# Eight more turns of the expert-weight ring, in tiles of G already multiplied

## The chip, the core and the metric

The kernel runs on one core of a Trainium2 chip. The metric is the device time of one execution in microseconds, as the median of several runs; lower is better. Before the change it is 1753.32 us (three runs, 1751.4 to 1754.4). The profile is of one further execution.

## The reference, cut to what matters

One layer of a hybrid encoder is computed for 384 tokens: 128 of eight short sequences and 256 of a prompt. The front of the layer (modulation, projections, RWKV-7 mixing, sparse attention, output projection) takes no part in the change. The layer ends in PEER, a mixture of 16,384 tiny experts with eight heads of sixteen picks each. For every token `n` with normed input `h` of 1024 numbers:

```python
act = gelu(einsum('nhkd,nd->nhk', peer_u[e], h))        # e: 8 x 16 picked experts of a token
out = einsum('nhk,nhkd->nd', g * act, peer_v[e])        # g: softmax of the picks' scores
x = x + g2 * out
```

## The kernel before

Tokens are handled in two ways. The 128 tokens of the short sequences (block 0) go the *sparse* way: for each of a token's 128 picks GpSimd gathers a row of `puv` (the expert's `u` and `v`, 2048 numbers a token, 1 MB for all 128 tokens) into one of three buffers of `raw` (`ring`, L1468). VectorE multiplies the `u` half by `h` and sums (L1593, called the product below), ScalarE turns the sum into a weighted activation (L1594, L1595), and VectorE adds that multiple of the `v` half to `acc` (L1599, the accumulation). One product and one accumulation are a pair; there are 128.

The 256 tokens of the prompt (blocks 1 and 2) go the *dense* way: all experts are computed, 128 tiles of 128 experts. `dense_u` (L1484) loads a tile of `puT`, 512 KB, multiplies it with the tokens on TensorE into the PSUM bank `fx` and puts the gelu into `G[:, j]` for the first 76 tiles, or into `gA` or `gO` for the later 52. A stage in between (`weights`, L1403) multiplies the tiles of G by the routing weights, and writes the weights of the later tiles to DRAM. In the last stage `dense_v` (L1507) loads a tile of `pv`, 512 KB, and multiplies it by the tile of G (or by `gA`, or by `gB` read back from DRAM, after GpSimd has multiplied it by the weights `Ws`), adding up in the four PSUM banks `bx`, `cp`, `dx`, `dx` over all 128 tiles. 36 of the 128 tiles (*whole*) are multiplied as they are, 8 passes each; 92 (*split*) are first cut into a high and a low half for three products of reduced precision: ScalarE makes `wh` and `Gh` (L231), VectorE `wl` and `Gl` (L235), and TensorE runs 12 matmuls. The last 20 tiles are all split. Buffers: four of `wh`, three of `wl`, three of `Gh` and `Gl`.

`expert` (L1473) takes the buffer for a tile of `puT` or `pv` from the ring `w`, four buffers of 128 x 1024, and issues the load on SP's DMA queue. The same queue carries the reads of `Ws` (L1556) and `gB` (L1515) and the writes of `y` (L1571), in order. The last stage is the loop at L1734 over the tiles in a fixed order `order`, which mixes later tiles in among the first 76. In each turn it draws about 0.62 gathers (`pull(SR[2])`), computes ahead the `dense_u` of later tiles (21 are left for this stage), and calls `dense_v`. A gather also waits for the matmuls of the tile five turns back (`self.pace`, L1735). At turn 122 it writes down the residual of block 0, which reads `acc`: two products on VectorE (L1569) and two additions on GpSimd (L1570). The two last tiles are multiplied bank by bank in `finish_v`, and blocks 1 and 2 follow with products and additions on VectorE. The buffers for these residuals are taken from the ring `raw` too, so they come free as the last gathers are used up and the output of block 0 is written.

What order the instructions have on each engine is not set by this code alone: the program is built with `schedule_with_timeline_sim=True`, that is, a scheduler lays the instructions of all engines along a simulated timeline, subject to their dependencies and buffers, and writes each engine's list in that order. At run time every engine takes its list strictly in order, waiting on semaphores.

Of the kernel before, what the change touches and what calls it, by code (L numbers as in the profile page):

```python
# [2 lines left out]

# [178 lines left out]
S0, PH = 30, 4  # L183
OFF = [j for j in range(NW, 128) if (j - NW + 1) * NB // (128 - NW) > (j - NW) * NB // (128 - NW)]
AHEAD = sorted(OFF + [j for j in range(NW, 128) if j not in OFF][:NA - 1])
LAST, EARLY = 126, 108
WB, EB = (4, 4, 3), 3
UENG, VENG, GENG, VN = 'v', 'v', 'g', 3
SENG = 'gv'
# [7 lines left out]
class K:  # L197
    def __init__(self, ctx, tc, I, O):
        self.ctx, self.tc, self.nc, self.I, self.O = ctx, tc, tc.nc, I, O
        self.uid = 0  # L200
        self.const = self.open(ctx, "const")
        self.stream = self.open(ctx, "stream")
        self.dram = self.open(ctx, "dram", space=bass.MemoryType.DRAM)
        self.nlo = 0
        self.lo_pattern = "v"

    def open(self, ctx, name, **kw):
# [1264 lines left out]

    def expert(self, src):  # L1473

        w = self.t([128, 1024], tag="w", bufs=WB[0], pool=self.stream)
        self.nc.sync.dma_start(w, src)
        return w

# [124 lines left out]
    def run(self):  # L1603
# [79 lines left out]
        def pull(rate):  # L1683
            sn[0] += rate
            while sn[0] >= 1:
                sn[0] -= 1
                next(sparse, None)
# [46 lines left out]
        for n, j in enumerate(order):  # L1734
            self.pace = self.vdone[n - 5] if n > 4 else None  # L1735
            pull(SR[2])
            while todo and sum(u not in OFF for u in gs) < NA - 1:
                u = todo.pop(0)
                gs[u] = self.dense_u(u)
            last.append(self.dense_v(j, gs.pop(j) if j >= NW else self.G[:, j], out, n))  # L1740
            if n == 122:
                for _ in sparse:
                    pass
                (a, b), (y, _) = self.ring(), self.ring()
                self.residual(0, [self.acc[:, c * 512:c * 512 + 512] for c in range(2)], self.gate2(0, a), self.x1_rows(0, b), y)
                (a, b), (c, y1), (y2, _) = (self.ring() for _ in range(3))
                g, x1, y = self.gate2(1, a), [self.x1_rows(1, b), self.x1_rows(2, c)], (y1, y2)
# [28 lines left out]
```

## Time and profile before

| | |
|---|---|
| median of three runs | 1753.32 us (1751.4 to 1754.4) |
| the profiled execution | 1746.57 us |
| its span, first to last instruction | 1744.3 us |
| granted TensorE clock, mean over the span | 0.983 |
| TensorE busy (PE) | 1672.7 us, 96% |
| VectorE busy (DVE) | 1352.8 us, 78% |
| ScalarE busy (ACT) | 747.1 us, 43% |
| GpSimd busy (POOL) | 557.4 us, 32% |
| moved by DMA | 437.22 MB, mean 251 GB/s |

In the rows of the profile PE is TensorE's matmul, PEld its load of weights (which overlaps PE), SPq the DMA queue of SP. `out<-in` names the written and the read tiles. A row of waits reads "engine, what waited <- what it waited for: us in total, times, the longest". In a row of the timeline stand the start and the length in us, the engine, the line and the operation, and in brackets how long the engine was idle before it and what ended that. The chain of waits lists pieces by start and length; a piece "DMA raw" runs from a gather's issue to the instruction that needed it. A DMA share of 1.00 means that all 16 DMA engines of the core were busy.

### The profile page before, as it was taken

Reading aid. Unit: us, or ns where it says so; the run is one execution under the profiler, and the core shown is the slowest. Engines: PE = TensorE matmul, PEld = TensorE weight load, DVE = VectorE, ACT = ScalarE, POOL = GpSimd, SP = SyncE. Lnnn points to the kernel's source line nnn. Section 1 sums busy time; section 2 is a strip of 40 time slices with the busy share of each in tenths; the row PEclk is TensorE's granted clock in tenths of the full one; section 3 lists DMA queues with packets and bytes.
Section 4 is the critical chain, followed back from the end, with each engine's and each line's share of the span. In section 5 each row is a group of like instructions: output and inputs, shape, how many; then the busy total and the mean of one; then the engine's idle time right before and its main releaser. Section 6 shows DMA issues by size and latency. Waiting matters only on the chain.

```text
span 1744.3 us, 33104 instructions
## 1 busy us (share of the span) xinstructions
PE 1672.7 (96%) x12376; PEld 1410.9 (81%) x12376; DVE 1352.8 (78%) x2905; ACT 747.1 (43%) x1666; POOL 557.4 (32%) x621
## 2 busy tenths in 40 slices
PE   6999999999999989999999989999999999999998
PEld 4998788878878877999887889999976667767766
DVE  4548788878858865566999998899958777878787
ACT  4443343334343333444323254577853343343344
POOL 2434243343323220035033223342243224333242
PEclk8999899999999999999999999999999999999999
DMA  8543653455365365755498989996579999999995
GB/s 301 165 139 100 196 176 89 146 171 162 104 204 158 96 207 191 257 184 198 126 360 315 370 318 373 387 340 240 176 259 388 346 346 382 382 359 377 349 377 213
DMA packets 173048, 437.22 MB, mean 251 GB/s; under 512 B 46036, under 2 KB 86612, under 8 KB 156504
## 3 DMA queue, kind: packets, MB, share of 16 engines
q1 hardware_dynamic: 154456, 300.89, 50.9%
q0 software_dynamic: 18432, 134.23, 19.9%
q8 instruction: 97, 1.59, 0.4%
q14 instruction: 63, 0.52, 0.1%
HBM read 403.75 MB, written 31.30 MB: 249 GB/s over the span
## 4 chain that ended last, share of the span: by engine, by line
PE 66%; DVE 15%; DMA 9%; issue 4%; ACT 3%; POOL 2%; SPq 0%; DVEq 0%; POOLq 0%; ACTq 0%
PE mm L227 25%; PE fx L227 14%; PE dx L227 11%; PE cp L227 7%; PE bx L227 7%; DMA raw<-in_puv,pe 3%; DVE raw L1593 2%; DVE acc L1599 2%; DVE wl L235 2%; DMA w<-in_pv 2%; DMA w<-in_w_ada 1%; ACT wh L231 1%; DVE psi L1323 1%; DVE ps L1324 1%; DMA w<-in_puT 1%
## 5 line engine op out<-in xcount | busy, mean ns | idle before, releaser
L235 DVE TENSOR_TENSOR wl<-w,wh 128x1024 fp32r<-128x1024 f32 (+1 forms) x274 | 345.7, 1271 | 107.1 <-ACT wh L231 68.0
L231 ACT ACTIVATE wh<-w 128x1024 fp32r<-128x1024 f32 (+1 forms) x282 | 294.9, 1052 | 152.3 <-PE mm L227 71.0
L1586 POOL DMA_INDIRECT raw<-in_puv,pe x128 | 175.2, 1369 | 434.8 <-PE dx L227 159.4
L227 PE MATMUL fx<-h2h,wl 128*128 128x256 f32 x688 | 195.2, 284 | 4.3 <-DVE wl L235 4.3
L227 PE MATMUL fx<-h2h,wh 128*128 128x256 f32 x688 | 196.8, 286 | 1.3 <-ACT wh L231 1.1
L227 PE MATMUL fx<-h2l,wh 128*128 128x256 f32 x688 | 193.1, 281 | 0.0
L1599 DVE SCALAR_TENSOR_TENSOR acc<-raw,dots,acc 128x1024 f32<-128x1024 f32 x127 | 166.6, 1311 | 15.9 <-ACT dots L1595 15.6
L1593 DVE SCALAR_TENSOR_TENSOR raw<-raw,sh 128x1024 f32<-128x1024 f32 x128 | 159.3, 1245 | 18.5 <-DMA raw<-in_puv,pe 14.9
L227 PEld LDWEIGHTS fx<-h2h,wl 128*128 128x128 f32 x688 | 129.9, 189 | 7.3 <-DVE wl L235 6.5
L227 PEld LDWEIGHTS fx<-h2h,wh 128*128 128x128 f32 x688 | 129.8, 189 | 5.0 <-ACT wh L231 2.7
L227 PEld LDWEIGHTS fx<-h2l,wh 128*128 128x128 f32 x688 | 129.9, 189 | 2.0 <-issue 1.5
L227 PE MATMUL mm<-LTh,wh 128*128 128x384 f32 (+2 forms) x352 | 123.7, 352 | 1.6 <-ACT wh L231 1.1
L227 PE MATMUL mm<-LTl,wh 128*128 128x384 f32 (+2 forms) x352 | 122.1, 347 | 1.1 <-POOL LTl L488 1.1
L227 PE MATMUL mm<-LTh,wl 128*128 128x384 f32 (+2 forms) x352 | 122.6, 348 | 0.0
L1594 ACT ACTIVATE dots<-dots 128x1 f32<-128x1 f32 x128 | 25.7, 200 | 189.9 <-DVE raw L1593 189.5
L227 PE MATMUL mm<-h2f,w 128*128 128x256 f32 x464 | 105.4, 381 | 0.0
L227 PE MATMUL mm<-wh,LTh 128*128 128x256 f32 x336 | 99.0, 295 | 1.6 <-ACT qx L891 1.6
L227 PE MATMUL mm<-wl,LTh 128*128 128x256 f32 x336 | 99.9, 297 | 0.0
L227 PE MATMUL mm<-wh,LTl 128*128 128x256 f32 x336 | 98.8, 294 | 0.0
L227 PEld LDWEIGHTS mm<-h2f,w 128*128 128x128 f32 x464 | 87.5, 190 | 12.4
L227 PE MATMUL fx<-h2f,w 128*128 128x256 f32 x336 | 78.0, 385 | 0.0
L227 PEld LDWEIGHTS mm<-LTh,wh 128*128 128x128 f32 (+2 forms) x352 | 66.4, 189 | 7.1 <-issue 2.0
(584 smaller groups left out, 4271.6 us busy)
## 6 DMA issues: line engine op xcount, KB each, us to landing
w<-in_puT SPq DMA_DIRECT2D x128, 512.0 KB
w<-in_pv SPq DMA_DIRECT2D x128, 512.0 KB
w<-in_w_in SPq DMA_DIRECT2D x70, 512.0 KB
w<-in_w_ada SPq DMA_DIRECT2D x48, 512.0 KB
cKT<-in_cKT SPq DMA_DIRECT2D x32, 256.0 KB
cV<-in_cV SPq DMA_DIRECT2D x32, 256.0 KB
w<-in_w_pq SPq DMA_DIRECT2D x16, 512.0 KB
d<-wst SPq DMA_DIRECT2D x8, 832.0 KB
```

Source lines behind the costliest of these rows:

```text
L227: return self.nc.tensor.matmul(out, l, r, start=start, stop=stop, skip_group_check=True, **kw)
L231: self.nc.scalar.activation(hi, src, AF.Copy)
L235: (self.nc.vector if eng == "v" else self.nc.gpsimd).tensor_tensor(lo, src, hi, op=OP.subtract)
L1323: nc.vector.max_index(si[:, half, h, 0:8], sv[:, half, h, 0:8], s[:, c])
L1324: nc.vector.match_replace(out=s2, in_to_replace=sv[:, half, h, 0:8], in_values=s[:, c], imm_value=MARK)
L1586: d = nc.gpsimd.indirect_dma_start(out=bass.AP(tensor=u.tensor, offset=u.offset, ap=[u.ap[0], [1, 2048]]), out_offset=None, in_=self.I["puv"],
L1593: nc.vector.scalar_tensor_tensor(u, u, 1.0, h2, op0=OP.mult, op1=OP.mult, accum_out=dot)
L1594: nc.scalar.activation(dot, dot, AF.Gelu_apprx_tanh)
L1599: nc.vector.scalar_tensor_tensor(acc, v, dot, acc, op0=OP.mult, op1=OP.add)
```

## The change

The ring gets further members. `slots` is a queue that holds None four times, for the four buffers of `w`. `expert` takes its first entry and puts it back at the end; None means a buffer of `w` as before, a number s the four tiles `G[:, 4s:4s+4]`, which together have a buffer's 128 x 1024 numbers. In the last stage, after the tiles up to j = 31 have been passed to `dense_v`, each full four of them adds its number to the queue, so that it grows from four to twelve entries. The queue is walked while the program is built.

```diff
--- before.py
+++ after.py
@@ -1,5 +1,6 @@
 
 import math
+from collections import deque
 from contextlib import ExitStack, nullcontext
 
 import numpy as np
@@ -183,7 +184,7 @@
 S0, PH = 30, 4
 OFF = [j for j in range(NW, 128) if (j - NW + 1) * NB // (128 - NW) > (j - NW) * NB // (128 - NW)]
 AHEAD = sorted(OFF + [j for j in range(NW, 128) if j not in OFF][:NA - 1])
-LAST, EARLY = 126, 108
+LAST, EARLY, SLOTS = 126, 108, 8
 WB, EB = (4, 4, 3), 3
 UENG, VENG, GENG, VN = 'v', 'v', 'g', 3
 SENG = 'gv'
@@ -202,6 +203,7 @@
         self.stream = self.open(ctx, "stream")
         self.dram = self.open(ctx, "dram", space=bass.MemoryType.DRAM)
         self.nlo = 0
+        self.slots = deque([None] * WB[0])
         self.lo_pattern = "v"
 
     def open(self, ctx, name, **kw):
@@ -1472,7 +1474,12 @@
 
     def expert(self, src):
 
-        w = self.t([128, 1024], tag="w", bufs=WB[0], pool=self.stream)
+        s = self.slots.popleft()
+        self.slots.append(s)
+        if s is None:
+            w = self.t([128, 1024], tag="w", bufs=WB[0], pool=self.stream)
+        else:
+            w = self.G[:, 4 * s:4 * s + 4].rearrange("p a b -> p (a b)")
         self.nc.sync.dma_start(w, src)
         return w
 
@@ -1738,6 +1745,8 @@
                 u = todo.pop(0)
                 gs[u] = self.dense_u(u)
             last.append(self.dense_v(j, gs.pop(j) if j >= NW else self.G[:, j], out, n))
+            if j < 4 * SLOTS and j % 4 == 3:
+                self.slots.append(j // 4)
             if n == 122:
                 for _ in sparse:
                     pass
```

The lines of the changed kernel stand 7 lower in this stage (L1593 is L1600 there, L1599 is L1606, L235 is L237, L1476 is L1483).

The scheduler writes another order for all engines from the first load into G on. On SP's DMA queue, early in the last stage, before the change (`w` is the ring, `Ws` and `gB` are read back from DRAM):

```order
L1476 DMA w_2983_15611<-in_pv 128x1024
L1476 DMA w_2990_15641<-in_puT 128x1024
L1476 DMA w_2995_15674<-in_pv 128x1024
L1556 DMA Ws_3128_16275<-d2173_11077 128x8x128
L1476 DMA w_3000_15696<-in_pv 128x1024
L1476 DMA w_3005_15714<-in_pv 128x1024
L1476 DMA w_3012_15743<-in_pv 128x1024
L1476 DMA w_3017_15765<-in_pv 128x1024
L1476 DMA w_3020_15779<-in_puT 128x1024
L1476 DMA w_3025_15812<-in_pv 128x1024
```

The same part after the change:

```order
L1483 DMA G_2172_11076<-in_pv 128x1024
L1563 DMA Ws_3113_16260<-d2173_11077 128x8x128
L1483 DMA w_3008_15739<-in_pv 128x1024
L1483 DMA w_3013_15761<-in_pv 128x1024
L1483 DMA w_3016_15775<-in_puT 128x1024
L1483 DMA G_2172_11076<-in_pv 128x1024 x3
L1483 DMA w_3027_15836<-in_pv 128x1024
L1522 DMA gB_3056_15975<-d2174_11078 128x256
L1483 DMA w_3039_15894<-in_pv 128x1024
L1483 DMA w_3046_15924<-in_puT 128x1024
```

Loads into `G` now stand among those into `w`, and the first reads of `gB` and `Ws` keep their places between them.

On VectorE, where the last gather is used. Before the change, from the product of the 128th gather (`raw_3633`) to the residual of block 0, which reads `acc`:

```order
L1593 SCALAR_TENSOR_TENSOR raw_3633_18583,dots_3634_18585<-raw_3633_18583,sh2_2289_11699 128x1024
L235 TENSOR_TENSOR wl_3642_18615<-w_3640_18612,wh_3641_18614 128x1024
L235 TENSOR_TENSOR Gl_3654_18664<-G_2172_11076,Gh_3653_18663 128x256
L235 TENSOR_TENSOR wl_3647_18637<-w_3645_18634,wh_3646_18636 128x1024
L1599 SCALAR_TENSOR_TENSOR acc_2290_11701<-raw_3633_18583,dots_3634_18585,acc_2290_11701 128x1024
L235 TENSOR_TENSOR wl_3652_18660<-w_3650_18657,wh_3651_18659 128x1024
L235 TENSOR_TENSOR Gl_3660_18689<-gB_3658_18685,Gh_3659_18688 128x256
L1569 TENSOR_TENSOR raw_3667_18727<-acc_2290_11701,raw_3666_18726 128x512 x2
L235 TENSOR_TENSOR wl_3657_18682<-w_3655_18679,wh_3656_18681 128x1024
```

Behind these rows come, before the residuals of the other blocks, six more `wl` and six more `Gl`, of dense tiles that are still to come. After the change, from the product of the 115th gather (`raw_3446`) on; `wl_3615` and `Gl_3618` belong to the last dense tile:

```order
L1600 SCALAR_TENSOR_TENSOR raw_3446_17979,dots_3447_17981<-raw_3446_17979,sh2_2289_11699 128x1024
L237 TENSOR_TENSOR wl_3611_18744<-G_2172_11076,wh_3610_18743 128x1024
L237 TENSOR_TENSOR Gl_3613_18749<-gA_3452_18023,Gh_3612_18748 128x256
L1606 SCALAR_TENSOR_TENSOR acc_2290_11701<-raw_3439_17950,dots_3440_17952,acc_2290_11701 128x1024
L237 TENSOR_TENSOR wl_3615_18754<-G_2172_11076,wh_3614_18753 128x1024
L237 TENSOR_TENSOR Gl_3618_18761<-gB_3616_18757,Gh_3617_18760 128x256
L1606 SCALAR_TENSOR_TENSOR acc_2290_11701<-raw_3446_17979,dots_3447_17981,acc_2290_11701 128x1024
L1600 SCALAR_TENSOR_TENSOR raw_3457_18046,dots_3458_18048<-raw_3457_18046,sh2_2289_11699 128x1024
L1606 SCALAR_TENSOR_TENSOR acc_2290_11701<-raw_3457_18046,dots_3458_18048,acc_2290_11701 128x1024
L1600 SCALAR_TENSOR_TENSOR raw_3463_18074,dots_3464_18076<-raw_3463_18074,sh2_2289_11699 128x1024
L1606 SCALAR_TENSOR_TENSOR acc_2290_11701<-raw_3463_18074,dots_3464_18076,acc_2290_11701 128x1024
L1600 SCALAR_TENSOR_TENSOR raw_3470_18110,dots_3471_18112<-raw_3470_18110,sh2_2289_11699 128x1024
```

Behind these rows come the products and accumulations of the gathers 118 to 128, then the three residuals, and no `wl` or `Gl` any more: 13 products, those of the gathers 116 to 128, stand behind VectorE's last operation for a dense tile, where before none did.

## The prediction

> **What bounds the kernel now.** I read the times first, then the profile in stretches, then who waited for whom on TensorE, ScalarE and the DMA queue, and last the timeline of the end. The change acts only in the last stage, from about 1285 us on. Here is that stage cut into pieces (span of the piece, then busy us and instructions of each engine, granted clock, DMA share, GB/s):
>
> ```profile
> 1285.00:1385.00 100.00, 97.04 (x417) 68.00 (x416) 73.12 (x87) 36.59 (x77) 39.52 (x34) 1.00 0.96 361
> 1385.00:1485.00 100.00, 97.89 (x425) 70.06 (x425) 78.36 (x91) 40.22 (x81) 36.84 (x29) 1.00 0.98 370
> 1485.00:1585.00 100.00, 97.27 (x428) 69.71 (x427) 78.94 (x94) 39.95 (x82) 31.45 (x28) 1.00 0.98 371
> 1585.00:1685.00 100.00, 95.71 (x403) 68.29 (x402) 77.16 (x94) 39.50 (x82) 33.00 (x26) 1.00 0.96 364
> ```
>
> TensorE is busy 96 to 98 of 100 us at a granted clock of 1.00, and the DMA engines 0.96 to 0.98 of the time: both nearly full. A busy TensorE need not run at its peak, so I check its pace. The timeline shows the first matmul of a split tile, and that of the next tile:
>
> ```profile
> 1690.62 0.39 PE L227 MATMUL bx<-wh,Gh 128*128 128x512 f32 x1
> ...
> 1693.34 0.39 PE L227 MATMUL bx<-wh,Gh 128*128 128x512 f32 x1
> ```
>
> A tile's 12 matmuls take 2.72 us, one each 0.227 us without a gap. What TensorE loses stands in its waits, first of the matmuls, then of the weight loads that run ahead of them (us in total, times, longest):
>
> ```profile
> PE bx L227 <- DVE wl L235: 5.7, 7, 1.5
> PE bx L227 <- ACT wh L231: 5.0, 7, 1.3
> PE fx L227 <- DVE wl L235: 1.8, 3, 0.8
> PE fx L227 <- ACT wh L231: 1.1, 1, 1.1
> ```
>
> ```profile
> PEld bx L227 <- DVE wl L235: 13.6, 17, 1.9
> PEld bx L227 <- ACT wh L231: 12.8, 15, 2.1
> ...
> PEld fx L227 <- ACT wh L231: 2.9, 6, 1.5
> PEld fx L227 <- DVE wl L235: 2.8, 5, 1.0
> ```
>
> The matmuls wait 13.6 us in all, the weight loads 32.1 us (most of it under a matmul that still runs). ScalarE, which makes `wh`, waits for loads 21.1 us, and the DMA queue waits for ring buffers that VectorE or TensorE still reads:
>
> ```profile
> ACT wh L231 <- DMA w<-in_pv: 12.0, 12, 2.5
> ACT wh L231 <- DMA w<-in_puT: 9.1, 5, 4.6
> ```
>
> ```profile
> SPq L1476 <- DVE wl L235: 153.6, 72, 5.9
> SPq L1476 <- PE dx L227: 99.1, 28, 7.2
> ```
>
> So the four-buffer ring holds the DMA queue up for some 250 us, but only 13.6 us of that arrive at TensorE.
>
> **The change, part by part.** *The deeper ring.* No instruction and no byte is added or removed; the turns of the ring are settled while the program is built. A load into a slot of G now waits for the last reader of four tiles of G, and behind it on SP's queue stand the reads of `gB` and `Ws`, which GpSimd waits for; nothing in the waits of TensorE above comes from GpSimd, so I cost that at nothing (if that cover went, it would show as TensorE waiting). The gain cannot exceed what TensorE waits: 0 at one end, 32.1 us at the other (all waits of the weight loads), nearest the 13.6 us of the matmuls themselves. I take 9 us, since near the end VectorE is over-full by itself: in the new order 10 gathers stand among the splits of the last 20 tiles, 20 x (1.30 + 0.46) + 10 x 2.6 = 61 us against 20 x 2.72 = 54 us on TensorE, and the three buffers of `wl` cover only part of these 7 us. The durations are these:
>
> ```profile
> L235 DVE TENSOR_TENSOR wl<-w,wh 128x1024 fp32r<-128x1024 f32 x110 | 141.4, 1300 | 45.4 <-ACT wh L231 44.1 <-PE dx L227 1.2
> L1599 DVE SCALAR_TENSOR_TENSOR acc<-raw,dots,acc 128x1024 f32<-128x1024 f32 x70 | 92.1, 1316 | 14.5 <-ACT dots L1595 14.3
> L1593 DVE SCALAR_TENSOR_TENSOR raw<-raw,sh 128x1024 f32<-128x1024 f32 x70 | 87.6, 1251 | 11.5 <-DMA raw<-in_puv,pe 7.9 <-issue 3.6
> L235 DVE TENSOR_TENSOR Gl<-G,Gh 128x256 fp32r<-128x256 f32 x53 | 24.5, 464 | 24.2 <-PE dx L227 11.6 <-ACT Gh L231 7.9 <-ACT dots L1594 4.5
> ```
>
> *The order.* This is the larger part, and the diff does not tell it. With more buffers in the ring the scheduler sets the dense tiles closer together, and the gathers fall behind them. In both programs 70 gathers' products are still to come in this stage. Before, the last of them stood ahead of ten more `wl` splits on VectorE; now 13 products and their 13 accumulations stand behind the very last `wl` and `Gl`, as the rows in the section on the change show. VectorE takes its instructions in order, so these 13 pairs cannot begin before the dense work is over, where before they lay beside TensorE's matmuls. What one pair costs is read from a gather late in the stage:
>
> ```profile
> 1691.69 1.22 DVE L1593 SCALAR_TENSOR_TENSOR raw<-raw,sh 128x1024 f32<-128x1024 f32 x1
> ...
> 1692.83 0.09 DVE L1593 DVE_READ_ACCUMULATOR raw<-raw,sh 128x1 f32 x1
> ...
> 1692.95 0.20 ACT L1594 ACTIVATE dots<-dots 128x1 f32<-128x1 f32 x1 [1.21 <-DVE raw L1593]
> ...
> 1693.19 0.29 ACT L1595 ACTIVATE dots<-dots,pg 128x1 f32<-128x1 f32 x1
> ...
> 1694.30 1.28 DVE L1599 SCALAR_TENSOR_TENSOR acc<-raw,dots,acc 128x1024 f32<-128x1024 f32 x1
> ```
>
> 1.22 + 0.09 + 0.20 + 0.29 + 1.28 = 3.08, and with the handovers of 0.03 to 0.06 us between them 3.2 us, since with two exceptions the new order puts nothing between a product and its accumulation. The pairs also need their data. The chain of waits has gathers from issue to product:
>
> ```profile
> 873.32 6.39 DMA raw<-in_puv,pe
> ...
> 909.70 10.12 DMA raw<-in_puv,pe
> ...
> 1696.35 12.82 DMA raw<-in_puv,pe
> ```
>
> The first of all gathers, which met the DMA engines idle, took 6.39 us, one among loads 10.12 to 12.82. The ring of `raw` has three buffers, so a gather comes at best every (6.39 + 3.2)/3 = 3.2 us, no slower than VectorE; loaded it would be (10.12 + 3.2)/3 = 4.4. In the tail there are no loads left, so I take 3.2. The bounds are 2.6 (VectorE's own work alone, 1.22 + 0.09 + 1.28) and 4.4.
>
> *The output.* The first block's residual needs the last accumulation, and the buffers of the other two blocks come free only behind it. Its rows, and those of the end:
>
> ```profile
> L1569 DVE TENSOR_TENSOR raw<-acc,raw x2: 689/689/689, 1715.6 to 1716.2; 128x512 f32<-128x512 f32 x2
> L1570 POOL TENSOR_TENSOR raw<-raw,raw x2: 1514/3633/5752, 1716.4 to 1722.1; 128x512 f32<-128x512 f32 x2
> ```
>
> ```profile
> 1733.31 1.22 DVE L235 TENSOR_TENSOR wl<-w,wh 128x1024 fp32r<-128x1024 f32 x1
> ...
> 1740.19 0.69 DVE L1570 TENSOR_TENSOR raw<-raw,raw 128x512 f32<-128x512 f32 x1
> ```
>
> Behind the last accumulation come one product (0.69), two additions on GpSimd (2 x 1.51, the shorter of the two seen, as VectorE is idle then; both seen make 7.2), eight VectorE operations of 0.69 for the other blocks (5.5) and the stretch from VectorE's last operation to the end of the span (1744.3 - 1740.9 = 3.4): 12.7 us, at most 16.9.
>
> *The sum.* VectorE ended its last `wl` at 1734.5. Less 9: 1725.5. One accumulation still open, 1.3: 1726.8. 13 pairs of 3.2 us, 41.6: 1768.4. The output, 12.7: 1781.1. Against the span of 1744.3 that is 36.8 us more. The profiled execution took 1746.57 us, 2.3 above its span, and the median of the runs shown is 1753.32, 6.8 above that; I add the difference to the median: 1790 us, 2.1% slower.
>
> **The rivals.** *The loads were not TensorE's brake.* ScalarE waited for loads, but VectorE was 77 to 79% busy and also held `wl` up, and the DMA engines are nearly full whoever waits. Then the 9 us stay: 1799. For it speaks the DMA share, against it the 21.1 us that ScalarE waited for loads. 0.18.
>
> *The gathers of the tail come slower than VectorE takes them.* GpSimd must issue each one while VectorE is busy with operations of two inputs in SBUF. One of the two additions on GpSimd above took 5.75 us beside VectorE's splits and the other 1.51 when VectorE had nothing to do, and gathers issue in 0.94 to 4.13 us:
>
> ```profile
> L1586 POOL DMA_INDIRECT raw<-in_puv,pe x70: 939/1119/4128, 1291.7 to 1696.3; - x70
> ```
>
> With 4.4 us per gather the tail grows by 13 x 1.2 = 16 us: 1806. The Trainium skill (SBUF — State Buffer, section SBUF: two separate sides) says that VectorE and GpSimd lock a shared pair of ports for a whole instruction and the other blocks, and that GpSimd then cannot write a gather's descriptors. By that rule each issue would take the 4.13 us seen once in place of 1.12, and (6.39 + 3.0 + 3.2)/3 = 4.2 us per gather give 1803; the two additions agree with it, the median issue of 1.12 us beside a VectorE that is 77% busy does not. 0.15.
>
> *Faster.* All 32.1 us of weight-load waits go, and the stretch in the first `bx` matmuls too:
>
> ```profile
> L227 PE MATMUL bx<-wh,Gh 128*128 128x512 f32 x92 | 45.7, 497 | 5.1 <-ACT wh L231 5.0
> ...
> L227 PE MATMUL cp<-wh,Gh 128*128 128x512 f32 x92 | 36.1, 392 | 0.0
> ```
>
> These are 92 x 0.105 = 9.7 us, together 41.8, and the pairs run at 2.6 us: 1734.5 - 41.8 + 1.3 + 33.8 + 12.7 = 1740.5, 3.8 us less than now, 1749.5. It decides where VectorE's last `wl` ends before 1696. Against it: the tile above runs without a gap. The Trainium skill (Perfetto Trace Analysis, section Optimization Strategy) says that a gap that repeats on the engine that should be full can mean too few buffers for the next tile; here the gaps of the matmuls add up to 13.6 us in 459. 0.05, of which 0.03 faster and 0.02 about as now.
>
> That the loads are not issued earlier at all is the first rival, since the tail stands in the program's order either way.
>
> **How the numbers follow.** The forecast has 0.62, the rivals 0.18, 0.15 and 0.05. The range begins at 1774: TensorE gives back 20 us in place of 9 and the pairs take 2.8 us (1790 - 11 - 5). It ends at 1808: the second rival, and the first with GpSimd's additions at their longer time and the pairs at 3.5 us (1799 + 4 + 4). What is left out is the third rival and the first two together. A measurement of this kernel can tell about 0.2%, 3.5 us, from no change. Every case but the third rival is slower by more: slower 0.95, same 0.02, faster 0.03.
>
> **What would show it.** Right: VectorE's last `wl` ends near 1725 of the span and 13 pairs follow, about 3.2 us apart, to 1768; TensorE's last matmul lies some 40 us ahead of the last accumulation; the matmuls' waits fall from 13.6 us to about 5; the DMA share falls in the last 50 us; the DMA queue's 153.6 us of waiting for `wl` shrink. Wrong in size: the last `wl` at 1734 (first rival), or VectorE waiting for `raw` between the pairs (second). Wrong in sign: the last `wl` before 1696.

## The result and the profile after

The changed kernel takes 1775.65 us, the median of six runs (1771.32 to 1782.69); six runs of the kernel before have a median of 1751.27 us. The ratio is 1.0128, 95% interval [1.0105, 1.0152]: slower by 1.3%, where 2.1% and 1790 us were forecast. The profiled execution took 1775.95 us, its span is 1773.9 us.

First the last stage in pieces, as it was shown of before (span of the piece, busy us and instructions of PE, PEld, DVE, ACT and POOL, granted clock, DMA share, GB/s):

```profile
1285.00:1385.00 100.00, 98.57 (x440) 72.22 (x439) 66.85 (x80) 36.82 (x74) 33.96 (x32) 1.00 1.00 387
1385.00:1485.00 100.00, 100.00 (x446) 73.55 (x445) 70.11 (x84) 41.60 (x77) 23.69 (x22) 1.00 0.94 352
1485.00:1585.00 100.00, 100.00 (x441) 72.55 (x440) 71.23 (x82) 40.40 (x76) 32.44 (x26) 1.00 0.92 335
1585.00:1685.00 100.00, 100.00 (x424) 74.44 (x423) 78.87 (x94) 44.87 (x83) 32.73 (x24) 1.00 0.92 337
1685.00:1745.00 60.00, 33.29 (x144) 26.52 (x142) 50.14 (x62) 18.58 (x46) 22.93 (x16) 0.80 0.66 237
```

TensorE is busy 100 of 100 us in three pieces, where it had 95.7 to 97.9. The DMA share is 1.00 in the first piece (0.96 before) and 0.92 to 0.94 in the next three (0.96 to 0.98 before): the dense tiles run faster there with fewer bytes beside them. From 1685 on TensorE has 33 us of work in 60. Second, TensorE's waits for the splits, for the stage to its end (us in total, times, longest):

```profile
PEld bx L229 <- ACT wh L233: 2.1, 4, 1.4
...
PE bx L229 <- ACT wh L233: 1.0, 1, 1.0
...
PEld bx L229 <- DVE wl L237: 0.9, 1, 0.9
...
PE bx L229 <- DVE wl L237: 0.4, 1, 0.4
```

The matmuls' 13.6 us of before are 1.4, the weight loads' 32.1 are 3.0. Third, VectorE's timeline from the last `wl` (L237) to its last operation:

```profile
1711.91 1.22 DVE L237 TENSOR_TENSOR wl<-G,wh 128x1024 fp32r<-128x1024 f32 x1
1713.05 0.42 DVE L237 TENSOR_TENSOR Gl<-gB,Gh 128x256 fp32r<-128x256 f32 x1
1713.38 1.28 DVE L1606 SCALAR_TENSOR_TENSOR acc<-raw,dots,acc 128x1024 f32<-128x1024 f32 x1
1714.58 1.22 DVE L1600 SCALAR_TENSOR_TENSOR raw<-raw,sh 128x1024 f32<-128x1024 f32 x1
...
1721.72 1.22 DVE L1600 SCALAR_TENSOR_TENSOR raw<-raw,sh 128x1024 f32<-128x1024 f32 x1
...
1730.17 1.28 DVE L1606 SCALAR_TENSOR_TENSOR acc<-raw,dots,acc 128x1024 f32<-128x1024 f32 x1 [0.60 <-ACT dots L1602]
1733.20 1.23 DVE L1600 SCALAR_TENSOR_TENSOR raw<-raw,sh 128x1024 f32<-128x1024 f32 x1 [1.75 <-DMA raw<-in_puv,pe]
...
1757.12 1.23 DVE L1600 SCALAR_TENSOR_TENSOR raw<-raw,sh 128x1024 f32<-128x1024 f32 x1 [2.39 <-DMA raw<-in_puv,pe]
...
1758.27 2.68 DVE L1606 SCALAR_TENSOR_TENSOR acc<-raw,dots,acc 128x1024 f32<-128x1024 f32 x2
1760.99 1.29 DVE L1576 TENSOR_TENSOR raw<-acc,raw 128x512 f32<-128x512 f32 x2
...
1769.13 1.29 DVE L1577 TENSOR_TENSOR raw<-raw,raw 128x512 f32<-128x512 f32 x2 [0.77 <-DMA raw<-d]
```

The last `wl` ends at 1713.1. Thirteen products and accumulations follow, from 1714.6 to 1761.0, 46.4 us or 3.57 each, and then 12.9 us of output to 1773.9. The end of the kernel is the tail that the order foretold, behind a dense part that ended earlier than forecast.

### The profile page after: what moved, and what is told of

The parts are those of the page before. It is cut to its first block, busy times and chain, and to the rows that moved or that the text cites. A ratio compares the mean times of both kernels' runs of the same rounds, so it can differ in the third digit from the quotient of the medians.

```text
span 1773.9 us, 33227 instructions
## 1 busy us (share of the span) xinstructions
PE 1664.8 (94%) x12376; PEld 1412.1 (80%) x12376; DVE 1354.5 (76%) x2905; ACT 750.9 (42%) x1666; POOL 549.8 (31%) x621
## 5 line engine op out<-in xcount | busy, mean ns | idle before, releaser
L1593 POOL DMA_INDIRECT raw<-in_puv,pe x128 | 177.3, 1385 | 501.9 <-DVE acc L1606 319.7
L237 DVE TENSOR_TENSOR wl<-w,wh 128x1024 fp32r<-128x1024 f32 x208 | 261.1, 1260 | 91.8 <-ACT wh L233 35.3
L233 ACT ACTIVATE wh<-w 128x1024 fp32r<-128x1024 f32 x216 | 226.9, 1053 | 152.0 <-PE mm L229 71.0
L1606 DVE SCALAR_TENSOR_TENSOR acc<-raw,dots,acc 128x1024 f32<-128x1024 f32 x127 | 163.5, 1287 | 21.4 <-ACT dots L1602 20.6
L1600 DVE SCALAR_TENSOR_TENSOR raw<-raw,sh 128x1024 f32<-128x1024 f32 x128 | 159.8, 1249 | 15.2 <-DMA raw<-in_puv,pe 15.1
L237 DVE TENSOR_TENSOR wl<-G,wh 128x1024 fp32r<-128x1024 f32 x66 | 84.9, 1288 | 47.3 <-issue 29.2
```

The source lines that it names most:

```text
L233: self.nc.scalar.activation(hi, src, AF.Copy)
L237: (self.nc.vector if eng == "v" else self.nc.gpsimd).tensor_tensor(lo, src, hi, op=OP.subtract)
L1593: d = nc.gpsimd.indirect_dma_start(out=bass.AP(tensor=u.tensor, offset=u.offset, ap=[u.ap[0], [1, 2048]]), out_offset=None, in_=self.I["puv"],
L1600: nc.vector.scalar_tensor_tensor(u, u, 1.0, h2, op0=OP.mult, op1=OP.mult, accum_out=dot)
L1606: nc.vector.scalar_tensor_tensor(acc, v, dot, acc, op0=OP.mult, op1=OP.add)
```

## The experiments

The forecast had the mechanism: a gain on TensorE against a tail of gathers. Two things were to be found out: where a gain of over 20 us in place of 9 comes from (the ring, or the 13 gathers that no longer lie beside the dense tiles), and what the tail costs by itself. As a measure of the dense part I use the end of VectorE's last `wl` in the span.

**Order and ring apart.** The first kernel keeps the ring of four and draws the gathers late, so that the scheduler leaves 13 products behind the last `wl`, as in the changed kernel (`LATE` is 12):

```diff
-SR, UR = (0.5, 0.5, 0.62), 0.5
+SR, UR = (0.5, 0.5, 0.48), 0.5
...
-                next(sparse, None)
+                if len(self.done) < 128 - LATE:
+                    self.done.append(0)
+                    next(sparse, None)
...
-            if n == 122:
-                for _ in sparse:
-                    pass
+            if n == 127:
+                with self.tc.issue_after(self.lo.ins):
+                    for _ in sparse:
+                        pass
```

> The kernel before, ring of four, with its gathers drawn late: the scheduler then leaves 13 products behind the last wl on VectorE, and sets the others about as the changed kernel does. Nothing is left out. Theory A (the deeper ring itself gave the dense tiles their 21 us, the order of the gathers costs the tail): the dense tiles gain nothing, VectorE's last wl ends near 1734 of the span, 13 pairs of 3.6 us and the output follow, span near 1734.5 + 1.4 + 46.4 + 12.9 = 1795. Theory B (the 21 us came from the 13 gathers that no longer lie beside dense tiles, and the ring gave nothing): last wl near 1713, span near 1774. In between, both have a share, by the place of the last wl.

The second keeps the ring of twelve, and an order edge on VectorE (no semaphore, both ends are on the same engine) puts each dense tile's splits behind the product drawn six turns earlier (`LAG` is 6):

```diff
-            last.append(self.dense_v(j, gs.pop(j) if j >= NW else self.G[:, j], out, n))
+            with self.tc.issue_after(pulled[n - LAG].ins) if n >= LAG else nullcontext():
+                last.append(self.dense_v(j, gs.pop(j) if j >= NW else self.G[:, j], out, n))
```

> The changed kernel, ring of twelve, with one order edge on VectorE for each dense tile: its instructions stand behind the last product drawn six turns earlier. Five wl stand behind the last product, before ten, after none. Nothing is left out. Theory A (ring gives 21 us to the dense tiles, order alone costs the tail): the last wl ends near 1713 with all gathers among the dense tiles, span near 1744.3 - 21 = 1723, matmul waits of a few us. Theory B (the 21 us came from the gathers that left the dense tiles): span near 1744, matmul waits near those of before, 13.6 us, DMA share 0.96 to 0.98 to the end.

`tail_ring4` took 1781.71 us, 1.0155 of before [1.0124, 1.0185]; `pinned_ring12` took 1737.0 us, 0.9912 [0.9883, 0.9942], faster than both kernels. VectorE's last `wl` in the late kernel with the ring of four, and TensorE's weight loads there:

```profile
1723.26 1.21 DVE L236 TENSOR_TENSOR wl<-w,wh 128x1024 fp32r<-128x1024 f32 x1
```

```profile
PEld bx L228 <- DVE wl L236: 8.4, 9, 1.9
...
PEld bx L228 <- ACT wh L232: 2.0, 2, 1.5
PEld fx L228 <- ACT wh L232: 1.6, 1, 1.6
...
PEld fx L228 <- DVE wl L236: 1.6, 3, 1.0
```

The same in the pinned kernel with the ring of twelve, in which the residual of block 0 follows the splits at once:

```profile
1720.96 1.21 DVE L238 TENSOR_TENSOR wl<-G,wh 128x1024 fp32r<-128x1024 f32 x1
1722.09 0.41 DVE L238 TENSOR_TENSOR Gl<-gB,Gh 128x256 fp32r<-128x256 f32 x1
1722.43 1.28 DVE L1577 TENSOR_TENSOR raw<-acc,raw 128x512 f32<-128x512 f32 x2
```

```profile
PEld bx L230 <- DVE wl L238: 9.1, 7, 2.2
...
PEld bx L230 <- ACT wh L234: 1.9, 3, 1.4
...
PEld fx L230 <- ACT wh L234: 1.5, 2, 1.2
...
PEld fx L230 <- DVE wl L238: 0.2, 1, 0.2
```

Theory A alone wanted 1795 and 1723, theory B alone 1774 and 1744; both kernels lie between. Before more could be said, the yardstick had to be looked at: the profiled execution of before, 1746.57 us, is 5 to 8 us faster than the medians of its runs.

**A second profile of before.**

> The kernel before, unchanged, for a second profile: its profiled execution of 1746.57 us lies 5 to 8 us below the medians of its runs, so the place of its last wl, 1734.5, may not be typical. Theory E (the two effects add up: the ring gives 12.3 us, the 13 late gathers 10.0, together 21.4): last wl near 1734 again where the span is near 1744. Theory F (the execution was a fast one and the missing 5 to 8 us lie in the last stage): a span near 1752 with the last wl near 1742, and then the ring alone gives near 20 us, the late gathers alone 17 to 20, both together only 29.

Its runs have a median of 1753.13 us (0.9991 [0.9972, 1.001]); the profiled execution took 1755.42 us, with a span of 1753.6. Its last `wl`, and TensorE's weight loads:

```profile
1742.71 1.22 DVE L235 TENSOR_TENSOR wl<-w,wh 128x1024 fp32r<-128x1024 f32 x1
```

```profile
PEld bx L227 <- ACT wh L231: 14.4, 15, 2.1
PEld bx L227 <- DVE wl L235: 13.0, 18, 1.9
...
PEld fx L227 <- DVE wl L235: 4.6, 6, 1.4
...
PEld fx L227 <- ACT wh L231: 3.8, 6, 1.5
```

The last `wl` ends at 1743.9 in an execution 2.3 us above the median, so theory F stands. Not all of the difference from the first profile is waits, though. TensorE's granted clock, the third number from the right in a row of pieces, falls twice in this stage, where the first profile has 1.00 in the same pieces; behind the pieces stand two matmuls of the second:

```profile
1369.00:1373.00 4.00, 3.37 (x15) 3.37 (x16) 3.40 (x5) 0.50 (x2) 0.00 (x0) 0.58 0.94 346
1691.00:1697.00 6.00, 5.50 (x13) 4.33 (x14) 5.39 (x7) 3.10 (x5) 1.53 (x3) 0.50 0.86 309
```

```profile
1692.52 0.63 PE L227 MATMUL bx<-wh,Gl 128*128 128x512 f32 x1
1692.95 0.63 PE L227 MATMUL cp<-wh,Gl 128*128 128x512 f32 x1
```

The matmuls start 0.43 us apart in place of 0.227. TensorE's busy time, times what the clock lacks to 1.00, makes 1.4 and 2.8 us, some 4 us for both falls, an estimate from these pieces. Waits of TensorE lie just ahead of both, but the first profile has waits as long (1.5 us) without a fall, so the cause is open. The changed kernel, `tail_ring4` and `pinned_ring12` show no fall before their last `wl`. The four kernels make a table (median us, end of the last `wl`, sum of the weight loads' waits for `wh` and `wl`):

| | gathers among the dense tiles | 13 behind them |
|---|---|---|
| ring of 4 | before: 1753.1, 1743.9, 35.8 | tail_ring4: 1781.7, 1724.5, 13.6 |
| ring of 12 | pinned_ring12: 1737.0, 1722.2, 12.7 | changed kernel: 1775.7, 1713.1, 3.0 |

The ring alone brings the dense tiles 21.7 us, the late gathers alone 19.4, both together 30.8: they do not add up, as they use up the same waits (and the same falls of the clock). Against the first profile, with 12.3, 10.0 and 21.4, they would add, so the medians have to decide: if the two added, the changed kernel would take 1737.0 + 1781.7 - 1753.1 = 1765.6 us, since what follows the last `wl` adds up within 0.4 us. It takes 1775.7, and the 10 us between are just clear of intervals of 4 to 5 us on each ratio. The order costs 27 us of time with the ring of four (1.55%) and 39 with the ring of twelve (1775.7 - 1737.0). Against the second profile the sum of the weight loads' waits moves somewhat more than the end of the last `wl`: -22.2 for -19.4, -23.1 for -21.7, -32.8 for -30.8.

**How deep a ring.** The changed kernel with two more buffers in place of eight (`SLOTS` = 2), free and pinned:

> The changed kernel with two more buffers in place of eight (ring of six); 6 products stand behind the last wl. Nothing is left out. Theory A (the ring gives the dense tiles their time): if two buffers are enough for all of it, last wl near 1713 and a tail of 6 x 3.6, span near 1713.1 + 1.4 + 21.4 + 12.9 = 1749; with half of the gain 1759. Theory B (the gain follows the gathers that left the dense tiles, 6 of 13): last wl near 1725, span near 1725 + 1.4 + 21.4 + 12.9 = 1761.

> The pinned kernel with two more buffers in the ring in place of eight, and the gathers' products at the same places among the splits as there. If the ring has to hold back the loads of many tiles: most of the 15 us of the pinned kernel's advantage over before is lost, 1748 to 1752. If two buffers more cover the delay of a load (10 to 13 us at most in the traces, some four tiles): within 4 us of the pinned kernel's 1737.

The free one took 1756.92 us (1.0013 [0.9998, 1.0029]); the last `wl` ends at 1724.5, six pairs follow to 1744.0 and the output to 1756.8. That looks like theory B, which had the last `wl` at 1725. But the pinned one, with all gathers among the dense tiles, ends its last `wl` at 1722.7 and took 1738.68 us (0.9927 [0.9903, 0.9951]): the two buffers alone bring most of what the dense tiles gain here, and the six late gathers little but the tail, 18 us of it. Two more buffers give what eight give, within what can be measured.

**What sets the tail's pace.** Three more buffers for gathers in the changed kernel, in tiles of G (`RAWS` is 3):

```diff
-        r = self.t([128, 2048], tag="raw", bufs=EB, pool=self.peer)
+        s = self.rslots.popleft()
+        self.rslots.append(s)
+        if s is None:
+            r = self.t([128, 2048], tag="raw", bufs=EB, pool=self.peer)
+        else:
+            r = self.G[:, 8 * s:8 * s + 8].rearrange("p a b -> p (a b)")
...
+            if 4 * SLOTS <= j < 4 * SLOTS + 8 * RAWS and j % 8 == 7:
+                self.rslots.append(j // 8)
```

> The changed kernel with three more buffers for gathers (raw), in eight tiles of G each, from the middle of the last stage on; 13 products stand behind the last wl as in the changed kernel. Nothing is left out. If the three buffers of raw set the 3.57 us of a pair in the tail (a gather is issued only when the accumulation three before it is over): pairs near VectorE's own 2.6 to 3.2 us, tail 34 to 42 in place of 46.4 us, span 1761 to 1769. If the transfer of one gather is the limit (about 3.5 us each, one behind the other): pairs stay at 3.5, span near 1773. If GpSimd's issue is the limit: intervals of issues near 3.5 with GpSimd waiting for nothing.

It took 1761.62 us (1.0043 [1.0028, 1.0059]), 14 us less than the changed kernel. VectorE's timeline from the first product of the tail to its last operation:

```profile
1717.58 1.21 DVE L1606 SCALAR_TENSOR_TENSOR G<-G,sh 128x1024 f32<-128x1024 f32 x1
...
1746.45 0.69 DVE L1582 TENSOR_TENSOR raw<-bx,raw 128x512 f32<-128x512 f32 x1
...
1752.39 1.28 DVE L1612 SCALAR_TENSOR_TENSOR acc<-G,dots,acc 128x1024 f32<-128x1024 f32 x1
1753.58 1.29 DVE L1583 TENSOR_TENSOR raw<-raw,raw 128x512 f32<-128x512 f32 x2
1754.79 1.29 DVE L1582 TENSOR_TENSOR G<-acc,G 128x512 f32<-128x512 f32 x2
```

The 13 pairs and six of the eight residual operations of blocks 1 and 2 take 36.1 us, from 1717.6 to 1753.7; VectorE is hardly idle, and the output behind the last accumulation takes 8.1 us in place of 12.9. So the three buffers of `raw` set the 3.57 us; had the transfer of a gather set them, they would have stayed.

**Both orders kept, and six buffers.** The pinned kernel with the three more buffers of `raw`, and the pinned kernel with eight turns between a gather's drawing and the splits behind its product (`LAG` = 8):

> The pinned kernel with the ring of twelve and three more buffers of raw in tiles of G; nothing is left out. In the changed kernel the three buffers took the output from 12.9 to 8.1 us behind the last accumulation. If that part of the end is on the path here too: span 1735.2 - 4.8 = 1730. If the dense tiles end last (last wl at 1722.2, 13.0 us ahead of the end): between 1730 and 1735; deeper gathers may also start earlier and crowd the loads, then 1737 or more.

> The pinned kernel with eight turns in place of six between a gather's drawing and the tile whose splits stand behind its product; three wl stand behind the last product in place of five. If VectorE's list is tight in the pinned kernel (its matmuls wait 6.1 us for wl): a few us faster, 1732 to 1736. If the last accumulation, already 13 to 14.5 us ahead of the end there, sets the end: up to 5 us slower than 1737.

The first took 1737.39 us (0.9892 [0.9871, 0.9913]): no difference from the pinned kernel that can be told. That fits dense tiles that end last, but is not shown by its trace, in which the stage begins 8.8 us later than in the pinned kernel (first dense matmul at 1286.4 against 1277.6). The second took 1745.06 us (0.9949 [0.993, 0.9968]): slower than the pinned one, not faster. Its matmuls wait 8.5 us for `wl` (6.1 in the pinned one), but its last `wl`, at 1729.2, cannot be laid to that alone, since its first dense matmul already comes 3.7 us later (1281.3 against 1277.6). Why is open.

**By what a gather holds the dense tiles up.** A gather among them moves 1 MB and takes VectorE 2.6 us. I first halved the one, then the other, for the 70 gathers of the last stage. Both kernels with the ring of four also carry the pinned kernel's order edge (`LAG` is 6), which the lines shown leave out; no kernel has the ring of four, the edge and whole gathers. The gather of half the size also writes half the numbers, and the accumulation reads the same half as the product:

```diff
-                                                 in_=self.I["puv"],
+                                                 in_=self.I["puv"].rearrange("e (a d) -> (e a) d", a=2) if late else self.I["puv"],
```

> The kernel before, ring of four and its gathers among the dense tiles; each of the last stage's 70 gathers fetches 0.5 in place of 1 MB, so that the sparse result for block 0 is another; VectorE's work is as large as before. 35 MB less are moved than before, where moving 13 gathers out took 13 MB from the dense tiles and VectorE's last wl from 1734.5 to 1724.5. Theory D (gathers hold the dense tiles up through the DMA engines, by making the loads late): last wl at 1724 or earlier, down to the 1713 of the changed kernel, span 1734 to 1723, and ScalarE's waits for loads fall from 21 us to a few. Theory V (they hold them up through VectorE's 2.6 us each): last wl stays near 1734, span 1744.

```diff
+                c = slice(0, 1024 if self.pace is None else 512)
-                nc.vector.scalar_tensor_tensor(u, u, 1.0, h2, op0=OP.mult, op1=OP.mult, accum_out=dot)
+                nc.vector.scalar_tensor_tensor(u[:, c], u[:, c], 1.0, h2[:, c], op0=OP.mult, op1=OP.mult, accum_out=dot)
```

> The kernel before; in the last stage VectorE's products and accumulations take 512 in place of 1024 numbers each, so that the result for block 0 is another; the gathers are whole. VectorE's pairs fall from 2.6 to about 1.4 us. Theory D (the gathers hold the dense tiles up through the DMA engines): last wl stays near 1734, span 1744, less the part of the output that does not change. Theory V (through VectorE): last wl near 1724 or earlier, down to 1713, the matmuls' waits for wl (7.5 us) gone.

> The pinned kernel with the ring of twelve; products and accumulations of the last stage take 512 in place of 1024 numbers, so that the result for block 0 is another. With the ring of twelve the loads come early, and what is left in TensorE's waits is 6.1 us for wl and 2.0 for wh. If those are VectorE's load: last wl from 1722.2 to about 1715, span 1728. If the DMA engines at a share of 0.99 to 1.00 set the pace: last wl stays near 1722, span 1735.

With half the bytes the kernel took 1772.45 us, 1.01 [1.0076, 1.0123]: slower, against both theories. The waits of VectorE and of the DMA queue there:

```profile
DVE raw L1597 <- DMA raw<-in_puv,pe: 54.4, 23, 7.1
```

```profile
SPq L1477 <- DVE wl L236: 192.2, 56, 11.0
```

VectorE waits 54.4 us for gathers (9.1 in the second profile of before), with `wl` behind them in its list; the ring comes free late, and loads with it. The order is another, by the edge and perhaps by the smaller gathers; the stage begins 5.5 us later than in the second profile of before (1284.8 against 1279.4), and the granted clock falls to 0.50 six times in it. So this run tells nothing of what the bytes cost. With half the VectorE work the time was 1745.5 us, 0.994 [0.992, 0.996], 9 us less than before, with the edge as part of the change; its last `wl` ends at 1734.4. In the pinned kernel, where nothing else differs, it was 1732.53 us, 4.5 us less than with the whole work.

A cleaner test puts the work of gathers back into `tail_ring4`, where 13 had left: 13 loads of 1 MB, paced like gathers, into tiles of G that are done with; or 26 operations on VectorE.

```diff
             pull(SR[2])
+            if 20 <= n and n % 8 == 4 and n < 124:
+                k = n // 8
+                d = nc.gpsimd.dma_start(self.G[:, 0:8].rearrange("p a b -> p (a b)"), self.I["puv"][128 * k:128 * k + 128])
+                self.tc.add_manual_dep(d.ins, self.pace, mybir.DependencyInfo(
+                    mybir.DependencyClass.Sync, mybir.DependencyReason.DATA), reason="pace")
```

```diff
             pull(SR[2])
+            if 20 <= n and n % 8 == 4 and n < 124:
+                z = self.G[:, 0:8].rearrange("p a b -> p (a b)")
+                for _ in range(2):
+                    nc.vector.scalar_tensor_tensor(z[:, :1024], z[:, :1024], 1.0, z[:, 1024:], op0=OP.mult, op1=OP.mult)
```

> The kernel with the ring of four and 13 late gathers, and 13 loads of 1 MB more among the dense tiles, on the gathers' queue, paced as gathers are, into tiles of G that are multiplied and not read again; VectorE's list is the same but for single places (12 products behind the last wl). Theory D (a gather among the dense tiles holds them up by its megabyte on the DMA engines): last wl goes back from 1724.5 to about 1744, and the kernel takes some 19 us more than that one. Theory V (by its 2.6 us on VectorE): last wl stays near 1724, within 5 us of that kernel's time.

> The kernel with the ring of four and 13 late gathers, and 26 operations of a gather's size (1.2 to 1.3 us) more on VectorE among the dense tiles, on tiles of G that are multiplied and not read again; no byte more is moved. Theory D (DMA): last wl stays near 1724. Theory V (VectorE): last wl goes back to about 1744, some 19 us more than the kernel without them. Both in part: the halved VectorE work before gave 0.6%, 10 us, so some 5 to 10 us here, and the rest with the loads.

In the second of these kernels the scheduler laid all 26 operations between 1293 and 1391 us of the span; it took 1795.96 us (1.0245 [1.0208, 1.0282]), which is the price of a crowd. So the operations were paced like gathers (the same dependency as on the loads), without and with the loads, in the second case 12 of them:

> The kernel with the ring of four and 13 late gathers, and 26 operations more on VectorE, two for each eighth tile, paced as gathers are; the gathers stand at the same places as without them, no byte more is moved. Theory D (the DMA engines alone): within 4 us of that kernel's 1782. Theory V' (VectorE has a share beside the DMA's 12 us of 19): 1787 to 1791. If the crowd did not matter: 1796 as when they were all laid into the first 100 us.

> The same with 12 loads of 1 MB as well, on the gathers' queue: the DMA work and the VectorE work of 12 to 13 gathers beside the dense tiles, while 13 pairs still follow behind. If the two shares make up what gathers cost among the dense tiles: last wl near 1744 as in the second profile of before, some 19 us above the kernel without them, 1798 to 1803. If the shares overlap: no more than the dearer of the two alone, near 1793.

The last `wl` with the loads, with the spread operations, and with both, one kernel each:

```profile
1738.54 1.22 DVE L236 TENSOR_TENSOR wl<-w,wh 128x1024 fp32r<-128x1024 f32 x1
```

```profile
1723.79 1.23 DVE L236 TENSOR_TENSOR wl<-w,wh 128x1024 fp32r<-128x1024 f32 x1 [0.88 <-ACT wh L232]
```

```profile
1744.41 1.22 DVE L236 TENSOR_TENSOR wl<-w,wh 128x1024 fp32r<-128x1024 f32 x1
```

| | median us | ratio to before | first dense matmul | last `wl` | between them | weight loads' waits |
|---|---|---|---|---|---|---|
| tail_ring4 | 1781.71 | 1.0155 [1.0124, 1.0185] | 1278.0 | 1724.5 | 446.5 | 13.6 |
| with 26 operations, spread | 1785.83 | 1.0202 [1.0167, 1.0237] | 1275.3 | 1725.0 | 449.7 | 12.8 |
| with 13 loads | 1793.38 | 1.0217 [1.0188, 1.0246] | 1281.7 | 1739.8 | 458.0 | 26.6 |
| with both (12 loads) | 1802.13 | 1.0285 [1.0244, 1.0327] | 1281.7 | 1745.6 | 463.9 | 33.3 |

The place of the last `wl` is no fair measure here, as the stage begins at other times in the four traces, and the added loads are not the cause: the first is issued at 1344.5. Between the first dense matmul and the last `wl` the second profile of before has 464.5 us, so that the late gathers bring 18.0. Of these the loads alone take back 11.5 us (12 in the medians), the operations alone 3.2 (4 in the medians, with intervals that overlap), both together 17.4 (20 in the medians), nearly the whole. In each of the three traces the granted clock falls to 0.50 two or three times in the stage, by the same kind of estimate 3 to 5 us of these figures, and for the operations alone about the whole 3.2. So with a ring of four a gather holds the dense tiles up mainly by its megabyte, as far as a plain load stands for a gather; its VectorE work adds to that when the loads are late as well.

## Why the forecast was right in its sign and off in its size

**The tail: right.** The 13 pairs stand behind the last `wl` and `Gl`. `pinned_ring12` differs from the changed kernel by the order alone, and is 39 us faster, so it is shown that the order makes the slowdown and that the ring is a gain. Why the scheduler gives that order was only argued: its own timeline was not examined.

**"I take 9 us": the step that failed.** The dense tiles gained 21.4 us against the profile shown (1734.5 to 1713.1) and 30.8 against an execution near the median. Two errors are in it. The step took the matmuls' 13.6 us as the nearest row and said of the weight loads' waits that most of them lie "under a matmul that still runs". In the runs the gain lies between the two rows, nearer to the weight loads': against the first profile these fell by 29.1 us and the matmuls' waits by 12.2, for a gain of 21.4; against the second by 32.8 and 13.8, for 30.8. The weight loads' row is no exact measure: in `ring4_half_gather` it is 24.3 us, 11.5 less than in the second profile of before, and yet the way from the first dense matmul to the last `wl` is 4.4 us longer. And the sum had the tail pay for the 13 pairs, but gave the dense tiles nothing for being rid of them, though the DMA share of 0.96 to 0.98 was quoted. `tail_ring4` shows this at 19.4 us with a ring of four; beside the ring of twelve it is still 9.1 (1722.2 to 1713.1). The ring's part alone is 21.7. The 19.4 and the 21.7 are measured from the second profile, with the falls of the clock in it.

**"A gather comes at best every (6.39 + 3.2)/3 = 3.2 us": mis-sized.** The pairs took 3.57 us, 46.4 in place of 41.6. The rule behind it, that three buffers of `raw` set the pace, is what `raw_six` confirms. What the rule leaves out is the time from the accumulation that frees a buffer to the next gather's issue: 0.77 us for the gather issued at 1732.22, shown further below, as the accumulation at 1730.17 ends at 1731.45. With it a turn of a buffer is 0.77 + 6.39 + 3.2, or 3.45 us a pair. Ten of the 13 products waited less than 0.9 us for their gather or not at all, the others 1.00, 1.75 and 2.39 us, 8.4 us in all. The open accumulation and the output came as forecast (1.5 and 12.9 us for 1.3 and 12.7). With 1713.1 + 1.5 + 46.4 + 12.9 the span is 1773.9.

**"I add the difference to the median": wrong.** The 6.8 us by which the profile shown was faster than its median lie mostly in the last stage: from the first dense matmul to the last `wl` it has 457.9 us (1276.6 to 1734.5), the second profile 464.5 (1279.4 to 1743.9). Of these 6.6 us some 4 are the two falls of the granted clock, by the estimate above, and 1.6 waits of the matmuls (13.6 and 15.2; the weight loads' are 32.1 and 35.8). The changed kernel hardly has these waits, and no fall of the clock there; its own profiled execution is within 0.3 us of its median. Of the 14 us between forecast and median, 7 are this step, 12 less 5 the two above.

**The rivals.** That the loads were not TensorE's brake fell: the waits for `wh` and `wl` are gone, and the ring alone brings the dense tiles 21.7 us. That gathers come slower than VectorE takes them holds in kind, at 3.57 us and not 4.2 to 4.4, and by the buffers. GpSimd's share can be seen in two issues of the tail of the changed kernel, the first beside the product at 1721.72 shown above (it ends at 1722.94), the second while VectorE is idle between the rows at 1730.17 and 1733.20:

```profile
1722.08 1.68 POOL L1593 DMA_INDIRECT raw<-in_puv,pe  x1 [3.18 <-DVE acc L1606]
...
1732.22 0.94 POOL L1593 DMA_INDIRECT raw<-in_puv,pe  x1 [1.84 <-issue]
```

The issue beside the product took 0.74 us longer, where I had put 3.0. The Trainium skill (SBUF — State Buffer, section SBUF: two separate sides) says that VectorE and GpSimd share a pair of ports as an exclusive lock, which an operation with two inputs in SBUF takes only against a GpSimd operation that reads SBUF (the gather reads `pe`), and that the one that comes second is blocked for the other's whole instruction; the prediction left the condition out. The first row agrees, as what was left of the product is 0.86 us. The faster rival failed where it was put: the last `wl` did not end before 1696. But one row it was built on, the 32.1 us of weight loads' waits, did go almost whole. The other, the stretch in the first `bx` matmuls, did not (0.497 us each before):

```profile
L229 PE MATMUL bx<-wh,Gh 128*128 128x512 f32 x92 | 47.3, 515 | 1.0 <-ACT wh L233 1.0
```

**The signs named.** That TensorE's last dense matmul would lie some 40 us ahead of the last accumulation came true: it ends at 1718.3, 42.7 us ahead. That the DMA queue's waits for `wl` would shrink was wrong:

```profile
SPq L1483 <- DVE wl L237: 164.6, 58, 7.0
```

This is up to 1720 us of the span; before, it was 149.4 to the same point. With more buffers the queue runs further ahead, and waits there no less. A full queue that waits says nothing on who is late.

The pinned kernel shows that it was the interleaving that was lost, not the ring that was at fault. The Trainium skill (Perfetto Trace Analysis, section Optimization Strategy) says that where the most contended engine changes over time, interleaving those regimes can help; here the stage that fills TensorE and the DMA engines and the tail that leaves TensorE idle are such regimes, and 39 us between the two orders agree with it.

## What to carry to other kernels

A resource that is made larger can change the order that a scheduler writes, and the order can cost more than the resource brings: look at what stands behind the last instruction of the engine that ends last, and if something has moved there, pin it with an order edge on the same engine rather than give the resource up (here 1737 us in place of 1776, from 1753). When work is moved out of a full stage, price both ends, the tail that it makes and the stage that it leaves. And where matmuls queue behind weight loads, take the matmuls' waits as the least that can be won and the weight loads' waits as the most: here the gain of the dense tiles lay between them, nearer to the latter.

## What was not expected of the hardware

Single executions of the kernel before spread over 8 us and more with the same instructions (spans of 1744.3 and 1753.6 in the two profiles), and most of the difference lies in the stage in which the DMA engines are 0.96 to 0.98 busy (0.94 to 0.98 in the second profile); one profile is not a yardstick for 10 us there. The larger part of that stage's 6.6 us is TensorE's granted clock, which fell to 0.50 twice in one execution and not at all in the other; by the estimate above the two cost 1.4 and 2.8 us. Half the bytes for each gather went with a kernel 1% slower, whose order was another.
